# Two of a transformer block's branch projections as seven-product units, in place of plain products, in a one-core Trainium2 kernel

## The chip, the cores and the metric

The kernel runs on one core of a Trainium2 chip. The metric is the device time of one execution in microseconds (us), lower is better. The engines are called as the profile calls them: PE (TensorE, matrix products), PEld (its weight load), DVE (VectorE), ACT (ScalarE), POOL (GpSimd) and SP (SyncE, which here only issues transfers).

## The reference

One block of a streaming encoder on 256 positions of width 2048, in float32: a recurrence and a banded attention run side by side, their outputs are projected, gated and merged, and a squared-ReLU MLP follows. What matters here is the merge:

```python
z = u @ w_in                                   # u: rms_norm(x), 256 x 2048
...
gate_a, gate_b = jnp.split(jax.nn.sigmoid(gates), 2, axis=-1)
merged = gate_a * (y_a @ w_branch_a) + gate_b * (y_b @ w_branch_b)   # y: 256 x 1024, w_branch: 1024 x 2048
return merged @ w_out
...
h = h + jnp.square(jax.nn.relu(u @ w_up[l])) @ w_down[l]             # 2048 -> 8192 -> 2048
```

## The kernel before

Every matrix product is made from three fast ones. A weight tile `raw` of 128x1024 (two k tiles of 128 rows by 512 columns) comes from HBM, ACT casts its high part to `wh` (line 91), and DVE subtracts that to get the low part `wl` (line 92); the activations have been split in the same way. `mm3` (lines 140 to 142) then adds hi x wh, hi x wl and lo x wh into one PSUM bank. One such "split piece" therefore costs a load (issued by SP), a cast, a subtraction, and 12 matmuls of 128x512 (two k tiles, two halves m of the positions, three products each).

Large projections are made as a `Unit` of 1024 columns. In it 8 of the 16 k tiles are computed with seven block products in place of eight (a Strassen scheme): the weights' blocks A, B, C, D are combined on the way (`sums` on DVE: A+=B, later A+=C; `sent`: accumulating DMAs from POOL, B+=C and D+=A), and the activations' sums S2, S4, S5, S7 are made once by `combos`. Each of the seven products needs its own split piece, with only six matmuls per piece, since it serves one half m. The other k tiles are "plain" pieces with 12 matmuls, named `r<column half>_<k tile>`. A unit's four banks start from each other (`begun`: a copy on ACT), and two are corrected by `less` on DVE. `run` writes a unit's order; a unit's last plain pieces (`late`) run in the next unit, and the steps of other work (`steps`) are called at set places in it.

A piece is named after its unit, product and k tile: `gb0p11D0` is unit gb0, bank 11, block D, k tile 0; `gb0r1_8` is a plain piece. The order of the stages around the change is: gates `ga0`, `ga2` (with the attention's steps), gates `gb0`, `gb2`, the branches (`ba`, `bb`), the output projection `wo0`, `wo2`, the MLP's units `up00` to `up32` and `dn00` to `dn32`. The branches have 8 k tiles only. They are computed by `gemm2` in four rounds of 512 columns, for each round `ba` then `bb`, with four pieces of 12 matmuls each. DVE multiplies each result with its gate (line 1113), and adds the two (line 1124).

Program order is a proposal: a scheduler puts instructions of each engine into their final order by priorities (`tc.high_priority`), and each engine then runs its own list strictly in that order. So a waiting instruction holds everything behind it on that engine, and on SP or POOL every later transfer. Buffers: six `raw`, three `rawp`, two `rawd`, four each of `wh` and `wl`. From gb0 on there is a fifth `wh` and `wl` (`buf`, lines 204 to 207).

Of the kernel before, what the change touches and what calls it, by code (L numbers as in the profile page):

```python
# [50 lines left out]
def tile_hybrid_block(  # L51
# [5 lines left out]
    nc = tc.nc  # L57
# [86 lines left out]
    def lhs_of(lhs, kt, m):  # L144
        return [lhs[kt // 4][:, kt % 4, u, m * P:(m + 1) * P] for u in range(2)]
# [51 lines left out]


    homes = {}
    taken = {"wh": 0, "wl": 0}  # L200

    def buf(tag, what):

        if "fifth" in homes:
            taken[tag] += 1
        last = taken[tag] > 0 and taken[tag] % 5 == 0
        return (homes["fifth"] if last else wpool).tile([P, 2 * NC], F32R, name=f"{tag}_{what}", tag=tag, bufs=1 if last else 4)

    def piece(w, what, n0, k0, tag="raw"):

# [529 lines left out]
    def fours(t):  # L740
        return t.rearrange("p (k t) -> p k t", t=P)
# [35 lines left out]
            nc.vector.tensor_tensor(dst, acc, dst, op=ALU.add)  # L777

    LATE = [(12, 13), (14, 15)]
    ITEMS = [(1, (8, 9)), (1, (10, 11)), (0, (8, 9)), (0, (10, 11)), (0, (12, 13)), (0, (14, 15))] + [(1, ks) for ks in LATE]  # L780

    class Unit:


        def __init__(self, lhs, S, w, n0, what, done, kt0=0, apart=NC, steps=lambda: (), start=5, fresh=None, held=False, tail=False):
            self.lhs, self.S, self.w, self.n0, self.what, self.done = lhs, S, w, n0, what, done
            self.apart = apart
            self.kt0, self.make_steps, self.start, self.held, self.tail = kt0, steps, start, held, tail
            self.spread, self.fresh = fresh is not None, fresh or ()
            self.raw, self.dma, self.c, self.items, self.steps = {}, {}, {}, list(ITEMS), []  # L790

        def load(self, name):

            jj, n, tag = {"A": (0, 0, "raw"), "B": (0, 1, "raw"), "C": (1, 1, "raw"), "D": (1, 0, "rawd")}[name]
            self.raw[name] = [piece(self.w, f"{self.what}{name}{g}", self.n0 + n * self.apart, self.kt0 + 4 * jj + g, tag)
                              for g in (0, 2)]

        def load_item(self):

# [23 lines left out]
                    mm3(self.c[i], *left(g + a), wh[:, a], wl[:, a], first and not g + a, False)  # L823

        def block(self, m, jj):
            return lambda k: lhs_of(self.lhs(), k + 4 * jj, m)

        def comb(self, i):
            return lambda k: self.S()[i][k]
# [31 lines left out]
        def plain(self, n, ks, which=range(NM)):  # L861

            while self.steps and self.steps[0][0] <= ks[-1] // 4:
                self.steps.pop(0)[1]()
            if (n, ks) not in self.raw:
                self.load_item()
            with ExitStack() as es:
                if marks and not n and ks in LATE:
                    es.enter_context(tc.issue_after(marks[0].ins))
                wh, wl = parts(self.raw[n, ks], f"{self.what}r{n}_{ks[0]}")  # L870

            def half(m, c=slice(0, NC)):
                for a, k in enumerate(ks):
                    mm3(self.c["12"[m] + "12"[n]][:, c], *lhs_of(self.lhs(), k, m), wh[:, a, c], wl[:, a, c], False, k == KD - 1)

            for m in which:
                half(m)
            return half
# [16 lines left out]
    def run(u, then=None):  # L895

        def q():
            if late:
                late.pop(0)()

        def item(x):
            if x and x.items:
                x.load_item()

        if not u.raw:
            u.load("A")
            u.load("B")
            u.load("C")
            u.load("D")
        for _ in range(3 - sum(type(k) is tuple for k in u.raw)):  # L910
            item(u)
        at = iter(range(99))
        seconds = [lambda: u.product("12", "C", u.comb(4)), lambda: u.product("11", "D", u.block(0, 1))]
        if not late and not u.spread:
            seconds.reverse()
        u.bank("11")
        u.product("11", "A", u.block(0, 0), True)
        u.begun("21", "11")
# [12 lines left out]
        u.step(next(at))  # L931
        seconds[1]()
        with ExitStack() as es:
            if u.spread:
                es.enter_context(tc.issue_after(lows[-1].ins))
            u.sums("A", "C")
        u.sent("D", "A")
        u.step(next(at))
        u.plain(1, (8, 9))
        item(u)  # L940
        u.step(next(at))
        u.product("21", "A", u.comb(2))
        u1 = u.copy(token(f"u1_{u.what}"), "21")
        if then:
            with ExitStack() as es:
                if u.held:
                    es.enter_context(tc.issue_after(u.dma[0, (10, 11)].ins))
                then.load("A")
        u.step(next(at))
        u.plain(1, (10, 11))  # L950
        u.less("12", u1)
        u.residual("12")
        item(u)
        u.step(next(at))
# [17 lines left out]
        if then:  # L972
# [10 lines left out]
        u.plain(0, (12, 13))  # L983
        item(u)
        u.step(next(at))
        u.plain(0, (14, 15))
# [12 lines left out]


# [66 lines left out]

    ga, gb = [], []
    units = []
    for gates, c, col, what, fresh in ((ga, 0, C_GA, "ga", None), (ga, 2, C_GA, "ga", None), (gb, 0, C_GB, "gb", ("21",)), (gb, 2, C_GB, "gb", ())):  # L1070
# [254 lines left out]
```

## Time and profile before

| | us |
|---|---|
| median of three runs (lowest, highest) | 1368.17 (1367.55, 1371.06) |
| the profiled execution | 1367.7 |
| its span, first to last instruction | 1366.0 |
| PE busy | 1356.6 (99 %) |
| DVE, ACT, POOL busy | 1122.2, 948.5, 150.1 |
| mean granted TensorE clock | 0.998 |

A row of the busy-time part names an engine, its busy time, its share of the span and its number of instructions. A row of the windows view gives one stretch: its length, then for each engine busy time and number of instructions, the granted clock, the share of the DMA engines' time and the bytes per second. A row of the timeline gives start, duration, engine, line, operation, output and inputs, and in brackets how long the engine sat idle before it and what ended that. A matmul's shown duration (about 390 ns) overlaps the next one, so the distance of two starts is what a matmul costs; the same holds, by less, for DVE and ACT.

### The profile page before, as it was taken

The page shows a single profiled execution, that of the slowest core. Times are in us where ns is not written, and L with a number is a line of the kernel's source. Part 1 is how long each engine was busy: PE and PEld are TensorE (multiplying, and loading weights), DVE is VectorE, ACT ScalarE, POOL GpSimd, SP SyncE. Part 2 cuts the span into 40 slices and gives each one's busy share as a digit, 9 for nine tenths or more (in the row PEclk, how much of TensorE's full clock was granted, in tenths as well). Part 3 has the DMA queues.
Part 4 walks back from the last instruction along what each step waited for, and adds up shares of the span by engine and source line. Part 5 has one row for each costly group of instructions (what it writes and reads, how often), then busy time and mean ns, then how long its engine had stood idle before and what let it go on. Part 6 is the DMA issues. An engine that isn't in the chain of part 4 may idle for free.

```text
span 1366.0 us, 19039 instructions
## 1 busy us (share of the span) xinstructions
PE 1356.6 (99%) x6787; PEld 1123.0 (82%) x6787; DVE 1122.2 (82%) x1302; ACT 948.5 (69%) x1247; POOL 150.1 (11%) x231
## 2 busy tenths in 40 slices
PE   9999999999999999999999999999999999999997
PEld 8888888878778888888888888888888888888886
DVE  7888977887788775798998987789787888878885
ACT  6877765776777664456678766687666876668864
POOL 4000000111111000010121111100111002110210
PEclk9999999999999999999999999999999999999999
DMA  9655557788886996569899889998899888998892
GB/s 333 240 186 156 181 177 264 216 221 244 260 225 169 293 296 210 182 154 324 284 265 269 235 260 295 283 256 244 250 278 298 250 253 237 286 296 258 269 281 98
DMA packets 128895, 333.75 MB, mean 244 GB/s; under 512 B 11152, under 2 KB 12176, under 8 KB 128416
## 3 DMA queue, kind: packets, MB, share of 16 engines
q1 hardware_dynamic: 108080, 265.85, 56.2%
q0 software_dynamic: 20144, 66.14, 24.7%
q8 instruction: 53, 0.87, 0.2%
q10 hardware_dynamic: 576, 0.55, 0.1%
q14 instruction: 42, 0.34, 0.1%
HBM read 271.67 MB, written 10.49 MB: 207 GB/s over the span
## 4 chain that ended last, share of the span: by engine, by line
PE 99%; DMA 1%; ACT 0%; POOLq 0%; issue 0%; POOL 0%
PE acc_hq L182 2%; PE acc_hf L182 2%; PE tp_u L110 1%; PE acc_hg L142 1%; PE acc_hi L142 1%; PE acc_hg L140 1%; PE acc_bb L140 1%; PE acc_hi L141 1%; PE acc_hf L187 1%; PE acc_ba L142 1%; PE acc_hg L141 1%; PE acc_bb L142 1%; PE acc_ba L140 1%; PE acc_ba L141 1%; PE acc_hi L140 1%; PE acc_bb L141 1%
## 5 line engine op out<-in xcount | busy, mean ns | idle before, releaser
L182 PE MATMUL acc_hf<-act_x,wh_hf 128*128 128x512 f32 x128 | 40.9, 401 | 0.6 <-ACT wh_hf L91 0.6
L182 PE MATMUL acc_hq<-act_x,wh_hq 128*128 128x512 f32 x128 | 40.8, 399 | 0.2 <-ACT wh_hq L91 0.2
L91 ACT CAST wh_bb<-raw_bb 128x1024 fp32r<-128x1024 f32 x16 | 16.9, 1054 | 23.3 <-PE acc_ba L142 17.7
L92 DVE TENSOR_TENSOR wl_bb<-raw_bb,wh_bb 128x1024 fp32r<-128x1024 f32 x16 | 19.6, 1223 | 14.8 <-ACT wh_bb L91 14.8
L91 ACT CAST wh_ba<-raw_ba 128x1024 fp32r<-128x1024 f32 x16 | 16.9, 1053 | 19.9 <-PE acc_bb L142 13.8
L92 DVE TENSOR_TENSOR wl_ba<-raw_ba,wh_ba 128x1024 fp32r<-128x1024 f32 x16 | 19.6, 1223 | 10.8 <-ACT wh_ba L91 10.8
L187 PEld LDWEIGHTS acc_hf<-act_x,wl_hf 128*128 128x128 f32 x128 | 23.4, 189 | 5.7 <-DVE wl_hf L92 0.5
L187 PEld LDWEIGHTS acc_hq<-act_x,wl_hq 128*128 128x128 f32 x128 | 23.4, 188 | 5.2
L1220 POOL DMA_DIRECT2D hd<-y x24 | 26.2, 1171 | 1.8 <-ACT y L1219 1.3
L92 DVE TENSOR_TENSOR act_u<-tp_u,act_u 128x512 fp32r<-128x512 f32 x32 | 21.9, 684 | 4.7 <-ACT act_u L91 4.2
L140 PE MATMUL acc_bb<-wh_bb,act_yb 128*128 128x512 f32 x64 | 25.2, 393 | 0.0
L140 PE MATMUL acc_hg<-wh_hg,act_x 128*128 128x512 f32 x64 | 25.1, 392 | 0.0
L140 PE MATMUL acc_hi<-wh_hi,act_x 128*128 128x512 f32 x64 | 25.0, 391 | 0.0
L142 PE MATMUL acc_hg<-wh_hg,act_x 128*128 128x512 f32 x64 | 24.9, 390 | 0.0
L142 PE MATMUL acc_ba<-wh_ba,act_ya 128*128 128x512 f32 x64 | 24.9, 389 | 0.0
L142 PE MATMUL acc_hi<-wh_hi,act_x 128*128 128x512 f32 x64 | 24.9, 389 | 0.0
L141 PE MATMUL acc_hi<-wl_hi,act_x 128*128 128x512 f32 x64 | 24.9, 389 | 0.0
L141 PE MATMUL acc_hg<-wl_hg,act_x 128*128 128x512 f32 x64 | 24.9, 389 | 0.0
L140 PE MATMUL acc_ba<-wh_ba,act_ya 128*128 128x512 f32 x64 | 24.9, 389 | 0.0
L141 PE MATMUL acc_ba<-wl_ba,act_ya 128*128 128x512 f32 x64 | 24.9, 389 | 0.0
L141 PE MATMUL acc_bb<-wl_bb,act_yb 128*128 128x512 f32 x64 | 24.9, 389 | 0.0
L142 PE MATMUL acc_bb<-wh_bb,act_yb 128*128 128x512 f32 x64 | 24.9, 389 | 0.0
(1996 smaller groups left out, 5220.2 us busy)
## 6 DMA issues: line engine op xcount, KB each, us to landing
raw_hi<-in_w_in_n_dram SPq DMA_DIRECT2D x16, 512.0 KB, 4.2
raw_hg<-in_w_in_n_dram SPq DMA_DIRECT2D x16, 512.0 KB, 3.6
raw_ba<-in_w_branch_a_dram SPq DMA_DIRECT2D x16, 512.0 KB, 4.5
raw_bb<-in_w_branch_b_dram SPq DMA_DIRECT2D x16, 512.0 KB, 4.5
raw_hf<-in_w_in_t_dram SPq DMA_DIRECT2D x12, 512.0 KB, 4.1
raw_hq<-in_w_in_t_dram SPq DMA_DIRECT2D x12, 512.0 KB, 5.3
hd<-y POOLq DMA_DIRECT2D x24, 256.0 KB, 7.5
raw_aq<-in_w_in_t_dram SPq DMA_DIRECT2D x8, 512.0 KB, 4.5
```

What stands on the lines that cost most here:

```text
L91: casts[:] = [(copy or nc.scalar.copy)(hi, src)]
L92: low[:] = [nc.vector.tensor_tensor(lo, src, hi.bitcast(F32), op=ALU.subtract)]
L110: nc.tensor.transpose(tp[:, j, :], src[:, j * P:(j + 1) * P], ident)
L140: nc.tensor.matmul(acc, hi, wh, start=first, stop=False, skip_group_check=True)
L141: nc.tensor.matmul(acc, hi, wl, start=False, stop=False, skip_group_check=True)
L142: newest[:] = [nc.tensor.matmul(acc, lo, wh, start=False, stop=last, skip_group_check=True)]
L182: newest[:] = [nc.tensor.matmul(acc[cb], wh[:, cb * P:(cb + 1) * P], r.rearrange("p u t -> p (u t)"), start=kt == 0, stop=last)]
L187: newest[:] = [nc.tensor.matmul(acc[cb][:, 0:T], wl[:, cb * P:(cb + 1) * P], r[:, 0, :], start=False, stop=False)]
L1220: nc.gpsimd.dma_start(hd[n][m], t, accum_op=ALU.add)
```

## The change

The first 1024 columns of both branches become two units, `ba0` and `bb0`, of a new small size (`nkt=8`): four k tiles by seven products, in two pairs, and four by plain pieces. Per unit that is 7 product pieces of 6 matmuls and 4 plain pieces of 12, so 90 matmuls where there were 96, and 11 split pieces where there were 8. `ba0` and `bb0` are chained behind `gb2` by `run`. The last 1024 columns stay with `gemm2`.

- The activations' sums for both branches are made ahead: eight additions of 128x256 on DVE (line 1077, a step of gb0) and four of 128x512; in gb2 four splits into S5, S4, S2 and S7 follow. They need a home for four tiles, `ysum`.
- That home is the place of the fifth `wh` and `wl`, which are gone. All units from gb0 to the end have four.
- The gated results of the first 1024 columns are summed by four accumulating DMAs from POOL (line 1116, 256 KB each) in place of four additions on DVE.
- The transposes of the first two merged blocks (`turned`) both come behind the third round's `ba`.

```diff
-        if "fifth" in homes:
-            taken[tag] += 1
-        last = taken[tag] > 0 and taken[tag] % 5 == 0
-        return (homes["fifth"] if last else wpool).tile([P, 2 * NC], F32R, name=f"{tag}_{what}", tag=tag, bufs=1 if last else 4)
+        return wpool.tile([P, 2 * NC], F32R, name=f"{tag}_{what}", tag=tag, bufs=4)
...
+    ITEMS8 = [(1, (4, 5)), (0, (4, 5)), (0, (6, 7)), (1, (6, 7))]
...
             self.raw[name] = [piece(self.w, f"{self.what}{name}{g}", self.n0 + n * self.apart, self.kt0 + self.nkt // 4 * jj + g, tag)
                               for g in range(0, self.nkt // 4, 2)]
...
-        if not late and not u.spread:
+        if len(late) < 2 and not u.spread:
             seconds.reverse()
...
-        u.plain(1, (8, 9))
+        if not u.small:
+            u.plain(1, (8, 9))
...
-        u.plain(1, (10, 11))
+        u.plain(1, (4, 5) if u.small else (10, 11))
...
         if then:
             then.load("B")
             then.load("C")
+            if then.small:
+                then.load("D")
...
-        u.plain(0, (8, 9))
+        u.plain(0, (4, 5) if u.small else (8, 9))
...
-        u.plain(0, (10, 11))
+        u.plain(0, (6, 7) if u.small else (10, 11))
...
-            u.plain(1, LATE[1])
+            u.plain(1, (6, 7) if u.small else LATE[1])
...
+    def y_block(m, j):
+        a = ysums[m, j] = fours(homes["fifth"].tile([P, NC], F32, name=f"ysum{m}{j}", tag=f"raw5{'ABCD'[2 * m + j]}", bufs=1))
+        for i, y in enumerate((ya, yb)):
+            x = y[0][:, 2 * j:2 * j + 2, :, m * P:(m + 1) * P].bitcast(F32)
+            nc.vector.tensor_tensor(a[:, 2 * i:2 * i + 2], x[:, :, 0, :], x[:, :, 1, :], op=ALU.add)
+
+    def y_final(i):
+        if not y_steps:
+            y_steps.extend(combos(None, "y", tk, Sy, ysums))
+        y_steps[i]()
...
+                              lambda: [(KD, lambda i=i: y_final(i), at) for i, at in enumerate((3, 5, 7, 9))]) if c else (
+                              lambda: [(KD, lambda m=m, j=j: y_block(m, j), 5 + 2 * m + j) for m in range(NM) for j in range(2)]),
...
+    def gated(what):
+
+        def done(m, n, acc):
+            gate = (ga if what == "ba" else gb)[n][m]
+            nc.vector.tensor_tensor(gate, acc, gate, op=ALU.mult)
+            if what == "bb":
+                nc.gpsimd.dma_start(ga[n][m], gate, accum_op=ALU.add)
+
+        return done
+
+    for i, (y, w, what) in enumerate(((ya, w_branch_a, "ba"), (yb, w_branch_b, "bb"))):
+        units.append(Unit(lambda y=y: y, lambda i=i: {k: v[2 * i:2 * i + 2] for k, v in Sy.items()}, w, 0, f"{what}0", gated(what), nkt=8))
     for u, then in zip(units, units[1:] + [None]):
         run(u, then)
...
-    for n in range(4):
+    for n in range(2, 4):
...
-            if what == "ba" and n:
-                for _, f in turned(mT, n - 1, f"m{n - 1}", ga):
-                    f()
+            if what == "ba":
+                for i in range(2 if n == 3 else 0, n):
+                    for _, f in turned(mT, i, f"m{i}", ga):
+                        f()
```

The order that results differs at three places that matter below. The first is DVE at the start of unit gb0, from the second half of product 22A to the first plain piece r1_8. `raw_gb0A0<-raw_gb0A0,raw_gb0C0` is the sum A+=C. Before:

```order
L92 TENSOR_TENSOR wl_gb0p22A0_4490<-raw_gb0A0_4217,wh_gb0p22A0_4489 128x1024
L92 TENSOR_TENSOR wl_gb0p22A2_4500<-raw_gb0A2_4219,wh_gb0p22A2_4499 128x1024
L92 TENSOR_TENSOR wl_gb0p12C2_4524<-raw_gb0C2_4268,wh_gb0p12C2_4523 128x1024
L92 TENSOR_TENSOR wl_gb0p11D0_4534<-rawd_gb0D0_4349,wh_gb0p11D0_4533 128x1024
L92 TENSOR_TENSOR wl_gb0p11D2_4544<-rawd_gb0D2_4351,wh_gb0p11D2_4543 128x1024
L854 TENSOR_TENSOR raw_gb0A0_4217<-raw_gb0A0_4217,raw_gb0C0_4266 128x1024
L854 TENSOR_TENSOR raw_gb0A2_4219<-raw_gb0A2_4219,raw_gb0C2_4268 128x1024
L92 TENSOR_TENSOR wl_gb0r1_8_4558<-rawp_gb0r1_8_4396,wh_gb0r1_8_4557 128x1024
```

After (the eight additions of line 1077 stand further ahead, between the pieces 11A0 and 11A2, and the sum of line 759 behind them):

```order
L92 TENSOR_TENSOR wl_gb0p22A0_4490<-raw_gb0A0_4217,wh_gb0p22A0_4489 128x1024
L763 TENSOR_TENSOR ysum10_4675<-ysum00_4620,ysum10_4675 128x512
L92 TENSOR_TENSOR wl_gb0p22A2_4500<-raw_gb0A2_4219,wh_gb0p22A2_4499 128x1024
L764 TENSOR_TENSOR ysum00_4620<-ysum11_4694,ysum00_4620 128x512
L92 TENSOR_TENSOR wl_gb0p12C0_4514<-raw_gb0C0_4266,wh_gb0p12C0_4513 128x1024
L765 TENSOR_TENSOR ysum01_4653<-ysum01_4653,ysum00_4620 128x512
L92 TENSOR_TENSOR wl_gb0p12C2_4524<-raw_gb0C2_4268,wh_gb0p12C2_4523 128x1024
L92 TENSOR_TENSOR wl_gb0p11D0_4534<-rawd_gb0D0_4349,wh_gb0p11D0_4533 128x1024
L92 TENSOR_TENSOR wl_gb0p11D2_4544<-rawd_gb0D2_4351,wh_gb0p11D2_4543 128x1024
L850 TENSOR_TENSOR raw_gb0A0_4217<-raw_gb0A0_4217,raw_gb0C0_4266 128x1024
L850 TENSOR_TENSOR raw_gb0A2_4219<-raw_gb0A2_4219,raw_gb0C2_4268 128x1024
L92 TENSOR_TENSOR wl_gb0r1_8_4558<-rawp_gb0r1_8_4396,wh_gb0r1_8_4557 128x1024
```

Three of the four combining additions (`ysum`) stand between the subtractions, and 12C0, which before came ahead of 22A0, stands behind 22A2.

The second place is DVE in unit up00, from the subtraction of piece 11D2 to that of the first plain piece r1_8. `hw` and `act_h` are the normed MLP input of the blocks 2 and 3, scaled out of a transpose (`tp`) and then split. Before:

```order
L92 TENSOR_TENSOR wl_up00p11D2_6670<-rawd_up00D2_6473,wh_up00p11D2_6669 128x1024
L854 TENSOR_TENSOR raw_up00A2_6331<-raw_up00A2_6331,raw_up00C2_6401 128x1024
L92 TENSOR_TENSOR act_h2_6618<-hw_2_0_6624,act_h2_6618 128x4x128
L1150 TENSOR_TENSOR hw_2_1_6654<-tp_h21_6649,vt_76 128x512
L92 TENSOR_TENSOR wl_up00r1_8_6695<-rawp_up00r1_8_6510,wh_up00r1_8_6694 128x1024
L92 TENSOR_TENSOR wl_up00p21A0_6723<-raw_up00A0_6329,wh_up00p21A0_6722 128x1024
```

After:

```order
L92 TENSOR_TENSOR wl_up00p11D2_6734<-rawd_up00D2_6537,wh_up00p11D2_6733 128x1024
L850 TENSOR_TENSOR raw_up00A0_6393<-raw_up00A0_6393,raw_up00C0_6463 128x1024
L92 TENSOR_TENSOR act_h2_6682<-hw_2_0_6688,act_h2_6682 128x4x128
L1181 TENSOR_TENSOR hw_2_1_6718<-tp_h21_6713,vt_76 128x512
L850 TENSOR_TENSOR raw_up00A2_6395<-raw_up00A2_6395,raw_up00C2_6465 128x1024
L92 TENSOR_TENSOR act_h2_6682<-hw_2_1_6718,act_h2_6682 128x4x128
L1181 TENSOR_TENSOR hw_3_0_6753<-tp_h30_6748,vt_76 128x512
L92 TENSOR_TENSOR wl_up00r1_8_6759<-rawp_up00r1_8_6574,wh_up00r1_8_6758 128x1024
```

The first sum A+=C has moved behind 11D2 (before, it stood right behind 22A0), and the second half of `act_h2` and the first of block 3 now stand ahead of r1_8. On PE the transposes of block 3 (`tp_h30`) stand ahead of r1_8 in both; after one matmul for each of r1_8's two banks, `tp_h31` comes, which before had come behind all twelve.

The third place is SP, the queue of loads, in the branches. Before, where the branches' rounds had only plain loads:

```order
L216 DMA raw_ba10_5249<-in_w_branch_a_dram 128x2x512
L216 DMA raw_ba12_5267<-in_w_branch_a_dram 128x2x512
L216 DMA raw_ba14_5285<-in_w_branch_a_dram 128x2x512
L216 DMA raw_ba16_5303<-in_w_branch_a_dram 128x2x512
L216 DMA raw_bb10_5340<-in_w_branch_b_dram 128x2x512
L216 DMA raw_bb12_5358<-in_w_branch_b_dram 128x2x512
L216 DMA raw_bb14_5376<-in_w_branch_b_dram 128x2x512
```

After, in unit bb0 (`ba2`, `bb2` are the third round):

```order
L211 DMA rawp_bb0r1_4_5279<-in_w_branch_b_dram 128x2x512
L211 DMA rawp_bb0r0_4_5283<-in_w_branch_b_dram 128x2x512
L211 DMA rawd_wo0D0_5873<-in_w_out_dram 128x1024
L211 DMA rawp_bb0r0_6_5285<-in_w_branch_b_dram 128x2x512
L211 DMA raw_ba26_5521<-in_w_branch_a_dram 128x2x512
L211 DMA raw_bb20_5573<-in_w_branch_b_dram 128x2x512
L211 DMA rawp_bb0r1_6_5320<-in_w_branch_b_dram 128x2x512
L211 DMA raw_bb22_5591<-in_w_branch_b_dram 128x2x512
```

The last plain piece of bb0, `rawp_bb0r1_6`, stands behind `raw_ba26` and `raw_bb20`, whose buffers are those that bb0's blocks A and B leave: the first is free when the accumulating DMA D+=A has read it, and the second when product 21B has been split.

More of the change, by code (lines that the diff above doesn't have):

```diff
@@ L199, in tile_hybrid_block @@
     homes = {}
-    taken = {"wh": 0, "wl": 0}
     def buf(tag, what):
-        if "fifth" in homes:
-            taken[tag] += 1
-        last = taken[tag] > 0 and taken[tag] % 5 == 0
-        return (homes["fifth"] if last else wpool).tile([P, 2 * NC], F32R, name=f"{tag}_{what}", tag=tag, bufs=1 if last else 4)
+        return wpool.tile([P, 2 * NC], F32R, name=f"{tag}_{what}", tag=tag, bufs=4)
     def piece(w, what, n0, k0, tag="raw"):
@@ L779, in tile_hybrid_block, with __init__ @@
     LATE = [(12, 13), (14, 15)]
+    ITEMS8 = [(1, (4, 5)), (0, (4, 5)), (0, (6, 7)), (1, (6, 7))]
     ITEMS = [(1, (8, 9)), (1, (10, 11)), (0, (8, 9)), (0, (10, 11)), (0, (12, 13)), (0, (14, 15))] + [(1, ks) for ks in LATE]
     class Unit:
-        def __init__(self, lhs, S, w, n0, what, done, kt0=0, apart=NC, steps=lambda: (), start=5, fresh=None, held=False, tail=False):
+        def __init__(self, lhs, S, w, n0, what, done, kt0=0, apart=NC, steps=lambda: (), start=5, fresh=None, held=False, tail=False, nkt=KD):
             self.lhs, self.S, self.w, self.n0, self.what, self.done = lhs, S, w, n0, what, done
-            self.apart = apart
+            self.apart, self.nkt, self.small = apart, nkt, nkt < KD
             self.kt0, self.make_steps, self.start, self.held, self.tail = kt0, steps, start, held, tail
             self.spread, self.fresh = fresh is not None, fresh or ()
-            self.raw, self.dma, self.c, self.items, self.steps = {}, {}, {}, list(ITEMS), []
+            self.raw, self.dma, self.c, self.items, self.steps = {}, {}, {}, list(ITEMS if nkt == KD else ITEMS8), []
         def load(self, name):
             jj, n, tag = {"A": (0, 0, "raw"), "B": (0, 1, "raw"), "C": (1, 1, "raw"), "D": (1, 0, "rawd")}[name]
-            self.raw[name] = [piece(self.w, f"{self.what}{name}{g}", self.n0 + n * self.apart, self.kt0 + 4 * jj + g, tag)
-                              for g in (0, 2)]
+            self.raw[name] = [piece(self.w, f"{self.what}{name}{g}", self.n0 + n * self.apart, self.kt0 + self.nkt // 4 * jj + g, tag)
+                              for g in range(0, self.nkt // 4, 2)]
         def load_item(self):
@@ L825, in block @@
         def block(self, m, jj):
-            return lambda k: lhs_of(self.lhs(), k + 4 * jj, m)
+            return lambda k: lhs_of(self.lhs(), k + self.nkt // 4 * jj, m)
         def comb(self, i):
@@ L873, in half @@
                 for a, k in enumerate(ks):
-                    mm3(self.c["12"[m] + "12"[n]][:, c], *lhs_of(self.lhs(), k, m), wh[:, a, c], wl[:, a, c], False, k == KD - 1)
+                    mm3(self.c["12"[m] + "12"[n]][:, c], *lhs_of(self.lhs(), k, m), wh[:, a, c], wl[:, a, c], False, k == self.nkt - 1)
             for m in which:
@@ L971, in run @@
         u.residual("21")
-        if then:
+        if then and not then.small:
             then.load("D")
@@ L982, in run @@
         u.step(next(at))
[L983 to L986, printed above, removed]
+        if not u.small:
+            u.plain(0, (12, 13))
+            item(u)
+            u.step(next(at))
+            u.plain(0, (14, 15))
         marks.clear()
@@ L993, in rest @@
         def rest():
-            u.plain(1, LATE[1])
+            u.plain(1, (6, 7) if u.small else LATE[1])
             u.end(1)
-        late.append(lambda: u.plain(1, LATE[0]))
+        if not u.small:
+            late.append(lambda: u.plain(1, LATE[0]))
         late.append(rest)
@@ L1069, in tile_hybrid_block @@
     units = []
+    ysums, Sy, y_steps = {}, {}, []
+    def y_block(m, j):
[7 more added lines that the diff above has]
+        y_steps[i]()
     for gates, c, col, what, fresh in ((ga, 0, C_GA, "ga", None), (ga, 2, C_GA, "ga", None), (gb, 0, C_GB, "gb", ("21",)), (gb, 2, C_GB, "gb", ())):
@@ L1075, in done @@
             gates[c + n][m] = sigmoid(token(f"gate_{what}{c + n}{m}", tkb if what == "gb" else None), acc, m)
-        units.append(Unit(lambda: xT, lambda: Sx, w_in_t, col + c * NC, f"{what}{c}", done, steps=gate_steps.pop(0) if gate_steps else lambda: (), fresh=fresh, held=what == "gb" and not c))
+        units.append(Unit(lambda: xT, lambda: Sx, w_in_t, col + c * NC, f"{what}{c}", done,
+                          steps=gate_steps.pop(0) if gate_steps else (
+                              lambda: [(KD, lambda i=i: y_final(i), at) for i, at in enumerate((3, 5, 7, 9))]) if c else (
+                              lambda: [(KD, lambda m=m, j=j: y_block(m, j), 5 + 2 * m + j) for m in range(NM) for j in range(2)]),
+                          fresh=fresh, held=what == "gb" and not c))
     for i in range(2):
```

## Prediction

> **What bounds the kernel now.** I read the busy shares first, then the chain that ended last, then what PE waited for.
>
> ```profile
> PE 1356.6 (99%) x6787; PEld 1123.0 (82%) x6787; DVE 1122.2 (82%) x1302; ACT 948.5 (69%) x1247; POOL 150.1 (11%) x231
> PE 99%; DMA 1%; ACT 0%; POOLq 0%; issue 0%; POOL 0%
> PE ps_warm L81 <- DVE warm L79: 1.1, 1, 1.1
> PE acc_hf L182 <- ACT wh_hf L91: 0.6, 1, 0.6
> PE acc_hq L182 <- ACT wh_hq L91: 0.2, 1, 0.2
> ```
>
> PE is busy 99 % of the span, carries 99 % of the chain, and waited 1.9 us in all, at the very start. A matmul less is therefore time gained, if nothing new makes PE wait. Whether PE waits depends on how far DVE and ACT are ahead of it in making `wh` and `wl`. The windows show how full they are, from the gates' first units with the attention (250:420) to the MLP:
>
> ```profile
> 250.00:420.00 170.00, 169.99 (x838) 135.91 (x836) 141.13 (x161) 125.19 (x199) 20.26 (x34) 1.00 0.84 244
> 420.00:436.00 16.00, 16.00 (x81) 12.78 (x80) 11.73 (x12) 12.76 (x15) 1.75 (x2) 1.00 0.58 155
> 436.00:450.00 14.00, 14.00 (x63) 11.45 (x62) 12.71 (x12) 9.72 (x12) 1.69 (x2) 1.00 0.64 134
> 450.00:513.00 63.00, 63.00 (x280) 52.16 (x279) 46.16 (x41) 40.59 (x45) 3.38 (x4) 1.00 0.90 301
> 513.00:600.00 87.00, 87.00 (x398) 72.32 (x397) 62.55 (x72) 38.46 (x43) 1.38 (x2) 1.00 0.61 190
> 640.00:680.00 40.00, 40.00 (x185) 33.08 (x185) 38.35 (x44) 30.14 (x41) 6.21 (x11) 1.00 0.94 297
> 680.00:712.00 32.00, 32.00 (x151) 26.47 (x150) 31.55 (x37) 23.74 (x33) 6.83 (x9) 1.00 0.85 242
> 712.00:1366.00 654.00, 646.55 (x2923) 535.03 (x2921) 536.36 (x513) 464.66 (x570) 79.92 (x101) 1.00 0.89 258
> ```
>
> DVE (the third busy time) has 24 us free in the branches (513:600), 1.3 of 14 at the start of gb0, and 2.1 of 72 from 640 to 712. The last two are the tight places.
>
> **What it removes.** Two units lose 6 matmuls each. What one costs is read where ACT's casts follow the release of buffers, one plain piece of 12 matmuls apart:
>
> ```profile
> 516.48 1.05 ACT L91 CAST wh_bb<-raw_bb 128x1024 fp32r<-128x1024 f32 x1 [1.09 <-PE acc_ba L142]
> ...
> 530.08 1.05 ACT L91 CAST wh_ba<-raw_ba 128x1024 fp32r<-128x1024 f32 x1 [1.67 <-PE acc_bb L142]
> ```
>
> These are the first and last of six in a row: 13.60 us for 5 x 12 matmuls, 0.2267 us each. So 12 fewer are worth -2.72 us; that is the most that can be gained. (The Trainium skill, page "TensorE: Matmul & The Clock Gate", section "Back-to-back issue gap", gives columns / 2.4 GHz + 2.5 ns, 0.216 us for 512 columns; by that it would be -2.59 us. The row here is 5 % above it, and the sum goes by the row.)
>
> **What it adds in the branches.** The durations:
>
> ```profile
> L91 ACT CAST wh_ba<-raw_ba 128x1024 fp32r<-128x1024 f32 x16 | 16.9, 1053 | 19.9 <-PE acc_bb L142 13.8
> L92 DVE TENSOR_TENSOR wl_ba<-raw_ba,wh_ba 128x1024 fp32r<-128x1024 f32 x16 | 19.6, 1223 | 10.8 <-ACT wh_ba L91 10.8
> L842 DVE TENSOR_TENSOR acc_gb2c<-acc_gb2c,u_gb 128x512 f32<-128x512 f32 x2 | 1.4, 700 | 1.1 <-ACT u_gb L812 0.6 <-PE acc_gb2c L142 0.5
> L704 DVE TENSOR_TENSOR sb<-sb,rs 128x256 f32<-128x256 f32 x8 | 3.4, 422 | 0.2
> 437.56 0.57 ACT L812 COPY acc_gb0c<-acc_gb0c 128x512 f32<-128x512 f32 x1 [0.36 <-PE acc_gb0c L142]
> ```
>
> DVE gets 6 subtractions (7.3 us), 4 sums of the same size (4.9) and 4 corrections (2.8), and loses 4 additions of like size (2.7): +12.3, on 62.55 of 87 us. ACT gets 6 casts and 8 copies, 6 x 1.05 + 8 x 0.57 = +10.9, on 38.46. Both stay under 90 % of what is then 84 us, so PE covers them: 0. If a piece were late there, it would cost its own lateness once.
>
> The four gate sums by DMA are issued from bb0's end on, and their readers, the transposes, now stand behind the third round's `ba`, 48 matmuls or 10.9 us later. A like transfer is the 512 KB sum of 4.4 to 8.6 us, so it is covered; the transposes' buffers add perhaps 0.1.
>
> New is the queue on SP: bb0's last plain piece is loaded only behind `ba26`, which waits for the accumulating DMA D+=A.
>
> ```profile
> raw_bb<-in_w_branch_b_dram SPq DMA_DIRECT2D x16, 512.0 KB, 4.5
> L216 SPq DMA_DIRECT2D raw_ba<-in_w_branch_a_dram x16: 367/368/378, 479.7 to 563.2; - x16
> rawd_gb0D<-raw_gb0A POOLq DMA_DIRECT2D x2, 512.0 KB, 6.1
> rawd_gb2D<-raw_gb2A POOLq DMA_DIRECT2D x2, 512.0 KB, 8.6
> ```
>
> From bb0's product 11D, about when D+=A can go, to r1_6 PE has 66 matmuls, 15.0 us. Needed are 6.1 (gb0's, with DMA engines 0.6 busy as here) to 8.6 (gb2's, at 0.90), two issues of 0.37 on SP (the second row: shortest, median, longest, in ns), 4.5 for the load, and 1.05 + 1.22 for the split: 13.7 to 16.2. So between 1.3 of room and 1.2 late; I take 0.4.
>
> **What it adds in gb0.** Eight additions of 128x256 and four of 128x512 come onto DVE between 11A0 and r1_8. Back to back an operation costs less than its duration: one of 128x512 shows 0.68 and starts 0.60 ahead of the next (697.87 and 698.47, rows of up00 below), and so I estimate 0.42 - 0.08, say 0.33, for 128x256. 8 x 0.33 + 4 x 0.60 = 5.0 us.
>
> ```profile
> 423.09 1.22 DVE L92 TENSOR_TENSOR wl_gb0p11A<-raw_gb0A,wh_gb0p11A 128x1024 fp32r<-128x1024 f32 x1 [0.58 <-ACT wh_gb0p11A L91]
> 428.06 1.23 DVE L92 TENSOR_TENSOR wl_gb0p11A<-raw_gb0A,wh_gb0p11A 128x1024 fp32r<-128x1024 f32 x1 [0.76 <-ACT wh_gb0p11A L91]
> 433.50 1.23 DVE L92 TENSOR_TENSOR wl_gb0p22A<-raw_gb0A,wh_gb0p22A 128x1024 fp32r<-128x1024 f32 x1 [1.82 <-ACT wh_gb0p22A L91]
> 437.24 1.23 DVE L92 TENSOR_TENSOR wl_gb0p11D<-rawd_gb0D,wh_gb0p11D 128x1024 fp32r<-128x1024 f32 x1 [0.24 <-ACT wh_gb0p11D L91]
> 438.38 2.35 DVE L854 TENSOR_TENSOR raw_gb0A<-raw_gb0A,raw_gb0C 128x1024 f32<-128x1024 f32 x2
> 440.65 1.22 DVE L92 TENSOR_TENSOR wl_gb0r<-rawp_gb0r,wh_gb0r 128x1024 fp32r<-128x1024 f32 x1
> 442.84 0.39 PE L140 MATMUL acc_gb0c<-wh_gb0r,act_x 128*128 128x512 f32 x1
> ```
>
> Between the two pieces of 11A and 11D DVE idled 0.76 + 1.82 + 0.24 = 2.8 us, so r1_8's subtraction starts about 2.2 later, at 442.85, and is ready at 444.05. PE wants it at 442.84 + 0.23, and in the new order one hi x wh product of the other bank comes first, so at 443.3. That is 0.75 late; 0.8 with the hand-offs. Below: if the first idle stretch (0.58, ahead of 11A0) helps, 0.3. Above: if only the 1.82 is usable, 1.9. Behind r1_8 wait the subtractions of 21A on DVE, whose PE turn comes 12 matmuls on; they are not late for a second time. In gb2 four splits of 128x512 (0.68 us on DVE each) stand ahead of plain pieces where DVE has about 17 of 63 us free: 0.2, between 0 and 0.5.
>
> **What goes away: the fifth buffers.** From gb0 on a cast may start one piece later. A piece lasts 1.36 us (six matmuls) to 2.72 us, and its split takes 2.3 us, so a piece is late only where DVE has a queue. The window 250:420 is the same scheme with four buffers, with DVE at 83 % and ACT at 74 %, and PE idled 0.01 us in 170. The units behind 712 have DVE at 82 % and ACT at 71 %: 0 there. At the start of wo0, where the transposes' splits join in, 0.2 (0 to 0.5), and in the last unit 0.2 (0 to 0.5).
>
> **What is moved in up00.** DVE has no room here:
>
> ```profile
> 697.87 0.68 DVE L1150 TENSOR_TENSOR hw<-tp_h,vt 128x512 f32<-128x512 f32 x1
> 698.47 1.21 DVE L92 TENSOR_TENSOR wl_up00r<-rawp_up00r,wh_up00r 128x1024 fp32r<-128x1024 f32 x1
> 699.62 0.60 PE L110 MATMUL tp_h<-ident,h 128*128 128x128 f32 x4
> 699.97 0.48 PE L140 MATMUL acc_up00c<-wh_up00r,act_h 128*128 128x512 f32 x1
> 700.28 0.40 PE L141 MATMUL acc_up00c<-wl_up00r,act_h 128*128 128x512 f32 x1
> ```
>
> Before, r1_8's `wl` was ready at 699.68, 0.60 ahead of its use at 700.28. In the new order `hw` of block 3 stands ahead of it, and that reads the transposes `tp_h30`, whose matmuls begin at 699.62 and end at 700.22. Then 0.60 for `hw` and 1.22 for the subtraction: ready at 702.04. PE has two hi x wh products (0.45), the transposes `tp_h31` (0.35) and one product of 21A (0.23) to fill in, from 699.97 to 701.0. That is 1.0 late; I take 1.2, since `act_h` and a cast that ACT now makes later stand ahead as well. Below 0.5, if PE gets to the transposes earlier against DVE; above 2.2, if 21A's subtraction, behind two more operations of 0.60, is late too.
>
> **Sum.** -2.72 + 0.1 (transposes) + 0.4 (load of r1_6) + 0.8 (gb0) + 0.2 (gb2) + 0.4 (four buffers) + 1.2 (up00) = +0.4 us. The profiled execution took 1367.7 us (span 1366.0), so 1368.1; the median of the runs before, 1368.17, is 0.5 above the profiled one, and I keep 1368.1 as the time. What a measurement of this kernel can tell from no change is 0.3 %, 4.1 us; the whole gain lies within it.
>
> **Rivals.**
>
> *All is hidden.* The scheduler's order fits, and the small waits are not there: -2.7 to -2.0, so 1365.0 to 1365.7. For it speaks that PE idles nowhere in the trace, though DVE is at 99 % from 680 to 712; against it, that the lead at the two tight places is 1.2 and 0.60 us and the additions are larger. Chance 0.30.
>
> *Slower: the four buffers.* Behind the branches come 18 units (wo, up, dn). In each, eight product pieces stand in a row, 10.9 us of PE against 8 subtractions and 4 sums of 1.14 us from start to start (437.24 and 438.38), 13.7 of DVE. The lead from the plain pieces pays the 2.8 us, and with a buffer less the lead that can be held is smaller. If each unit then waits 0.4 us, that is 7.2, with the sum above 1375.3. It decides the sign from (4.1 - 0.4) / 18 = 0.2 us a unit. Against it: the window 250:420. For it: those units carry evictions that the earlier ones have not. Chance 0.11.
>
> *Slower: one transfer.* D+=A of bb0 takes 8.6 us and the load of r1_6 more than 4.5, as loads do in gb2, and PE stands for 3 us and more. The trace shows what the clock does when PE has little to do:
>
> ```profile
> 1355.00:1362.00 7.00, 3.55 (x22) 2.99 (x20) 3.07 (x7) 3.89 (x10) 1.13 (x4) 0.95 0.51 180
> 1362.00:1366.00 4.00, 0.00 (x0) 0.00 (x0) 0.00 (x0) 0.00 (x0) 0.00 (x0) 0.50 0.58 209
> ```
>
> Granted was 0.95, then 0.50, behind PE's last work. At half clock each 3 us of matmuls takes 3 more, so a wait of 3 to 3.5 us would cost some 6: 1373 to 1374. (The Trainium skill, the same page, section "What's actually happening", says that the clock halves after an idle window of about 3.4 us and returns after a busy one as long; no PE wait inside the kernel here is long enough to show it.) Chance 0.04.
>
> **How the numbers follow.** My forecast, small waits that give back about the gain, has 0.55, and its own range is 1365.8 to 1371.9 (each term at its lower, then at its upper end, the sum runs from -1.9 to +4.2). All hidden has 0.30, the two slower cases 0.15. The range that leaves out half of the slow cases and the lowest tail is 1365.0 to 1372.5. Faster by over 0.3 %, under 1364.1, is more than the 12 matmuls can give: 0.02. Slower by over 0.3 %, above 1372.3: 0.14. Within: 0.84.
>
> **What would show it.** PE's busy time and count fall by 12 matmuls between 503 and 600, with PE without idle there: the part is right. A PE wait for `wl_gb0r` of about 0.8 us near 443 and one for `wl_up00r` of about 1.2 near 698 show the two main terms; none there means that all is hidden. A wait for `wh_bb0r` shows the queue on SP; waits for `wl` of up and dn units, many and small, show the buffers. The forecast would be wrong above all if such waits recur in every unit.

## The result, and the profile after

The changed kernel takes 1380.68 us (median of five runs, 1378.05 to 1381.62) against 1368.43 before (1367.55 to 1371.06): the ratio is 1.0084, 95 % interval 1.0073 to 1.0095. It is 12.3 us slower, above the whole predicted range. The profiled execution has a span of 1379.9 us, 13.9 above that of before. The medians given below leave out two single executions: one of 3486.8 us of *plain loads ahead*, and one of 1507.83 us of the kernel before beside *sums later*.

The page's busy times and chain, and what PE waited for from ga2 on (waits of 0.4 us and more: total, times, longest):

```profile
PE 1360.5 (99%) x6775; PEld 1118.6 (81%) x6775; DVE 1138.0 (82%) x1328; ACT 959.6 (70%) x1265; POOL 155.5 (11%) x239
PE 50%; DMA 9%; DVE 4%; issue 4%; ACT 2%; POOL 1%; SPq 0%; POOLq 0%; ACTq 0%; DVEq 0%
DMA rawp_up10r<-in_w_up_dram 2%; DMA rawp_dn22r<-in_w_down_dram 1%; DMA rawp_dn12r<-in_w_down_dram 1%; DMA rawp_up30r<-in_w_up_dram 1%; PE acc_dn00c L142 1%; PE acc_dn00c L140 1%; PE acc_dn32c L141 1%; PE acc_dn32c L140 1%; PE acc_up02c L142 1%; PE acc_dn32c L142 1%; PE acc_wo0c L142 1%; PE acc_wo0c L141 1%; PE acc_up02c L140 1%; PE acc_wo0c L140 1%; PE acc_dn00c L141 1%
PE acc_dn30c L140 <- ACT u_dn L808: 1.4, 1, 1.4
PE acc_up10c L141 <- DVE wl_up10r L92: 1.2, 3, 0.8
PE acc_ga2c L140 <- ACT u_ga L808: 1.0, 1, 1.0
PE acc_up00c L141 <- DVE wl_up00r L92: 0.9, 1, 0.9
PE acc_dn02c L141 <- DVE wl_dn02r L92: 0.8, 2, 0.6
PE acc_up00c L141 <- DVE wl_up00p22A L92: 0.8, 1, 0.8
PE acc_up30c L141 <- DVE wl_up30r L92: 0.8, 1, 0.8
PE acc_up20c L141 <- DVE wl_up20r L92: 0.6, 1, 0.6
PE acc_gb0c L140 <- ACT acc_gb0c L808: 0.4, 1, 0.4
```

PE issued its 12 matmuls less, but its share of the chain fell from 99 % to 50 %: the chain now runs through loads of plain pieces (`rawp`) of up and dn units. Many of the waits are for a plain piece's `wl`, far behind the change. They are small, and a matmul's shown duration hides part of each, so PE's busy time rose by 3.9 us though it did less.

Where the time went is best read from each unit's length, the distance from its first matmul to the next unit's first matmul in the one profiled execution of each kernel (us; the branches, from gb2's first matmul to the end of `bb2`, are one row, because the units overlap there; the units from gb0 on that are not listed differ by less than 0.1, but for dn22, 0.35 longer after the change):

| | before | after | four buffers alone | plain loads ahead | fifth from wo2 | sums in gate slots | sums later |
|---|---|---|---|---|---|---|---|
| ga2 | 47.72 | 49.61 | 47.93 | 47.73 | 49.19 | 47.71 | 48.64 |
| gb0 | 35.68 | 36.45 | 36.41 | 36.88 | 36.59 | 37.03 | 35.68 |
| gb2 to bb2 | 113.30 | 111.60 | 114.34 | 111.83 | 111.62 | 110.69 | 110.67 |
| wo0 | 36.33 | 36.51 | 36.51 | 36.52 | 36.51 | 36.32 | 36.33 |
| up00 | 42.71 | 45.04 | 44.13 | 44.17 | 43.99 | 42.71 | 42.71 |
| dn02 | 40.80 | 41.69 | 41.61 | 40.80 | 40.80 | 40.80 | 40.80 |
| up10 | 40.80 | 43.05 | 42.11 | 40.80 | 40.80 | 40.80 | 40.80 |
| up12 | 42.83 | 43.29 | 43.33 | 42.81 | 42.83 | 42.81 | 42.83 |
| dn12 | 40.80 | 41.46 | 40.80 | 40.80 | 40.80 | 40.80 | 40.80 |
| up20 | 40.80 | 42.23 | 41.89 | 40.80 | 40.80 | 40.80 | 40.80 |
| up22 | 42.81 | 43.25 | 43.31 | 42.81 | 42.83 | 42.81 | 42.83 |
| up30 | 40.80 | 42.49 | 42.23 | 40.80 | 40.80 | 40.80 | 40.80 |
| up32 | 42.80 | 43.25 | 43.31 | 42.81 | 42.81 | 42.80 | 42.81 |
| dn30 | 42.71 | 44.40 | 44.39 | 44.23 | 42.73 | 42.71 | 42.73 |

The columns behind "after" are experiments told below. The branches are 1.7 us shorter after the change; from up00 to dn30 12.6 us are lost. ga2's 1.9 us are not the change's: PE's wait in ga2, between 410 and 420, comes ahead of the first instruction that stands otherwise (an ACT cast at 425.50), and *plain loads ahead*, which has the changed order there too, has 47.73.

One of the late plain pieces, in up10, by the timeline. First the kernel before: the first of D+=A's two transfers on POOL; SP's loads of the next unit's B, of r0_12, and of r0_14 with r1_12; ACT's casts of r0_12 and r0_14.

```profile
860.99 0.86 POOL L859 DMA_DIRECT2D rawd_up10D<-raw_up10A  x1 [7.12 <-DVE wl_up10p11D L92]
868.98 5.63 SPq L216 DMA_DIRECT2D raw_up12B<-in_w_up_dram  x2
874.71 0.42 SPq L216 DMA_DIRECT2D rawp_up10r<-in_w_up_dram  x1
876.33 1.55 SPq L216 DMA_DIRECT2D rawp_up10r<-in_w_up_dram  x2
880.44 1.05 ACT L91 CAST wh_up10r<-rawp_up10r 128x1024 fp32r<-128x1024 f32 x1 [1.07 <-DMA rawp_up10r<-in_w_up_dram]
884.33 1.05 ACT L91 CAST wh_up10r<-rawp_up10r 128x1024 fp32r<-128x1024 f32 x1 [2.83 <-DMA rawp_up10r<-in_w_up_dram]
```

The same after; the last two rows are what SP waited for (total, times, longest), before between 836 and 896, after between 840 and 900.

```profile
868.50 0.85 POOL L855 DMA_DIRECT2D rawd_up10D<-raw_up10A  x1 [0.61 <-DVE wl_up10p11D L92]
878.01 5.59 SPq L211 DMA_DIRECT2D raw_up12B<-in_w_up_dram  x2
883.69 0.42 SPq L211 DMA_DIRECT2D rawp_up10r<-in_w_up_dram  x1
885.35 1.94 SPq L211 DMA_DIRECT2D rawp_up10r<-in_w_up_dram  x2
890.01 1.05 ACT L91 CAST wh_up10r<-rawp_up10r 128x1024 fp32r<-128x1024 f32 x1 [4.71 <-DMA rawp_up10r<-in_w_up_dram]
893.91 1.05 ACT L91 CAST wh_up10r<-rawp_up10r 128x1024 fp32r<-128x1024 f32 x1 [2.85 <-DMA rawp_up10r<-in_w_up_dram]
SPq L216 <- DMA rawd_up10D<-raw_up10A: 8.1, 2, 4.8
SPq L211 <- DMA rawd_up10D<-raw_up10A: 11.0, 2, 6.2
```

up10's first matmul is at 851.38 before and at 855.87 after. Against it, D+=A goes 9.6 us in before and 12.6 after, since the pieces that it waits for are split later with four buffers; the next unit's B loads, whose buffers D+=A frees, hold SP until 23.2 and 27.7; and r0_12, behind them in SP's order, is loaded 23.3 and 27.8 us in. Its cast comes 29.1 and 34.1 us in. PE came to the piece 35.4 us in before (its first matmul at 886.74); a cast and a subtraction are 2.3. Before there were 4 us to spare, after PE waits. Already before, both casts waited for a load and not for a free `wh`, so any delay of the loads went straight into this lead.

### The profile page after: what moved, and what is told of

Same layout as the page of the kernel before. It is cut to its first block, busy times and chain, and to the rows that moved or that the text cites. A ratio compares the mean times of both kernels' runs of the same rounds, so it can differ in the third digit from the quotient of the medians.

```text
span 1379.9 us, 19077 instructions
## 1 busy us (share of the span) xinstructions
PE 1360.5 (99%) x6775; PEld 1118.6 (81%) x6775; DVE 1138.0 (82%) x1328; ACT 959.6 (70%) x1265; POOL 155.5 (11%) x239
## 4 chain that ended last, share of the span: by engine, by line
PE 50%; DMA 9%; DVE 4%; issue 4%; ACT 2%; POOL 1%; SPq 0%; POOLq 0%; ACTq 0%; DVEq 0%
DMA rawp_up10r<-in_w_up_dram 2%; DMA rawp_dn22r<-in_w_down_dram 1%; DMA rawp_dn12r<-in_w_down_dram 1%; DMA rawp_up30r<-in_w_up_dram 1%; PE acc_dn00c L142 1%; PE acc_dn00c L140 1%; PE acc_dn32c L141 1%; PE acc_dn32c L140 1%; PE acc_up02c L142 1%; PE acc_dn32c L142 1%; PE acc_wo0c L142 1%; PE acc_wo0c L141 1%; PE acc_up02c L140 1%; PE acc_wo0c L140 1%; PE acc_dn00c L141 1%
## 5 line engine op out<-in xcount | busy, mean ns | idle before, releaser
L187 PEld LDWEIGHTS acc_hf<-act_x,wl_hf 128*128 128x128 f32 x128 | 23.2, 188 | 5.8 <-DVE wl_hf L92 0.7
L92 DVE TENSOR_TENSOR wl_hf<-raw_hf,wh_hf 128x1024 fp32r<-128x1024 f32 (+2 forms) x21 | 20.4, 970 | 5.7 <-ACT wh_hf L91 5.6
L187 PE MATMUL acc_hf<-act_x,wl_hf 128*128 128x256 f32 x128 | 24.7, 280 | 0.0
L187 PE MATMUL acc_hq<-act_x,wl_hq 128*128 128x256 f32 x128 | 24.6, 279 | 0.0
L100 POOL TENSOR_TENSOR ro<-os,mhalf 128x4 f32<-128x4 f32 x4 | 4.4, 1098 | 166.5 <-DVE os L99 163.5
L92 DVE TENSOR_TENSOR wl_hg<-raw_hg,wh_hg 128x1024 fp32r<-128x1024 f32 x16 | 19.4, 1215 | 3.0 <-ACT wh_hg L91 3.0
L182 PEld LDWEIGHTS acc_hf<-act_x,wh_hf 128*128 128x128 f32 x128 | 19.8, 189 | 1.6 <-DVE wh_hf L91 1.1
L695 ACT ACTIVATE sb<-sb,mx 128x128 f32<-128x128 f32 (+1 forms) x32 | 14.3, 449 | 9.6 <-DVE mx L692 9.4
L182 PEld LDWEIGHTS acc_hq<-act_x,wh_hq 128*128 128x128 f32 x128 | 19.8, 189 | 0.9 <-ACT wh_hq L91 0.4
L1240 ACT ACTIVATE r<-r 128x512 f32<-128x512 f32 x32 | 20.2, 631 | 0.5
L92 DVE TENSOR_TENSOR wl_hq<-raw_hq,wh_hq 128x1024 fp32r<-128x1024 f32 (+2 forms) x21 | 20.2, 970 | 0.4 <-ACT wh_hq L91 0.2
```

The costliest lines, as they stand in the source:

```text
L92: low[:] = [nc.vector.tensor_tensor(lo, src, hi.bitcast(F32), op=ALU.subtract)]
L100: nc.gpsimd.tensor_tensor(dst, ms, mhalf[:, :width], op=ALU.pow)
L182: newest[:] = [nc.tensor.matmul(acc[cb], wh[:, cb * P:(cb + 1) * P], r.rearrange("p u t -> p (u t)"), start=kt == 0, stop=last)]
L187: newest[:] = [nc.tensor.matmul(acc[cb][:, 0:T], wl[:, cb * P:(cb + 1) * P], r[:, 0, :], start=False, stop=False)]
L695: nc.scalar.activation(s[:, j, d], s[:, j, d], AF.Exp, bias=mx[:, b, j:j + 1], accum_out=sums[:, b, j:j + 1])
L1240: nc.scalar.activation(t, t, AF.Square)
```

## The experiments

Theory 1 was that chain of transfers; theory 2 the mechanism of the prediction's slower rival, DVE's lead through eight product pieces; theory 3 that the new units upset what follows.

**Four buffers alone.** The kernel before, with this edit and nothing else:

```diff
-        if "fifth" in homes:
-            taken[tag] += 1
-        last = taken[tag] > 0 and taken[tag] % 5 == 0
-        return (homes["fifth"] if last else wpool).tile([P, 2 * NC], F32R, name=f"{tag}_{what}", tag=tag, bufs=1 if last else 4)
+        return wpool.tile([P, 2 * NC], F32R, name=f"{tag}_{what}", tag=tag, bufs=4)
```

> The kernel before with the fifth wh and wl taken away and nothing else changed. Theory 1 (loads): without the fifth buffers each product piece is split some 3 us later against PE, so the accumulating transfer D+=A goes later, SP stands on the next unit's B loads that wait for it, and the plain loads behind them come late; PE waits in the up and dn units. Theory 2 (DVE): with a buffer less DVE cannot hold its lead through eight product pieces. By both the time is 1368.4 + 12 to 15, so 1380 to 1383, with the losses in up00, up10, up20, up30 and the dn units. Theory 3 (the branches): the new units' transfers and additions upset what follows; by it this kernel takes 1368 to 1370.

1381.25 us, 1.0086 of before (1.0073 to 1.0099). The lost buffer alone costs as much as the whole change did; theory 3 falls as the cause of the loss. Its column also has +0.73 in gb0 and +1.04 in gb2 to bb2, where there are no branch sums at all. From wo2's first matmul on, the order of every engine and queue is the same here as after the change, up00's included, so what is lost there is lost by the four buffers and the order that the scheduler makes for them. Even so the two columns differ by up to 0.9 us in a unit (9.3 against 12.6 us from up00 to dn30): that is how far one profiled execution can be read.

**Plain loads ahead.** The changed kernel, where in the up and dn units the next unit's B loads are issued behind r0_12 and r0_14:

```diff
         if then:
-            then.load("B")
+            with ExitStack() as es:
+                if u.what[:2] in ("up", "dn"):
+                    es.enter_context(tc.issue_after(u.dma[0, (14, 15)].ins))
+                then.load("B")
             then.load("C")
```

> The changed kernel, four buffers, where in the up and dn units the next unit's B loads are issued behind the unit's own plain loads r0_12 and r0_14; the order of PE, DVE, ACT and POOL is the same row by row. Theory 1: the waits for r0_12 and r0_14 go, which are most of the 11 us lost from up00's end on: 1371 to 1375. Theory 2: SP's order does not matter, 1379.5 to 1382.

1372.25 us, 1.0024 (1.0014 to 1.0035): 8.4 us less than the changed kernel, with four buffers and with the order of PE, DVE, ACT and POOL unchanged. So most of the loss is SP's order behind a late transfer, theory 1, and theory 2 fails as the main cause. Here is up10 again, POOL, SP and ACT (its first matmul is at 852.88):

```profile
864.33 0.95 POOL L855 DMA_DIRECT2D rawd_up10D<-raw_up10A  x1
867.91 10.58 SPq L211 DMA_DIRECT2D rawp_up10r<-in_w_up_dram  x3
878.54 0.46 SPq L211 DMA_DIRECT2D raw_up12B<-in_w_up_dram  x1
883.00 1.05 ACT L91 CAST wh_up10r<-rawp_up10r 128x1024 fp32r<-128x1024 f32 x1 [1.18 <-PE acc_up10c L142]
885.72 1.05 ACT L91 CAST wh_up10r<-rawp_up10r 128x1024 fp32r<-128x1024 f32 x1 [1.67 <-PE acc_up10c L142]
```

Three plain loads, those of r0_12 and r0_14 among them, are ahead of `raw_up12B`, and the casts wait for PE to free a `wh`, no longer for a load. D+=A still goes late, 11.4 us in: 1.8 of the 3.0 us that it lost after the change come with the four buffers themselves, and the rest with the late pieces of the unit before. The column shows 40.80 for up10, up20, up30, dn02 and dn12. What is left is 1.2 in gb0, 1.2 in gb2 (against the last column), 1.5 in up00 and 1.5 in dn30; for the first three theory 2 is not excluded.

dn30 has, by the trace, the same cause on other queues (no run moves this load alone). There ACT must scale `wf`, the final norm's weights, ahead of a copy that PE waits for, and `wf`'s load stands on POOL behind D+=A. After:

```profile
1295.74 0.85 POOL L855 DMA_DIRECT2D rawd_dn30D<-raw_dn30A  x1 [1.96 <-DVE wl_dn30p11D L92]
1296.28 0.87 POOL L1297 DMA_DIRECT2D wf<-in_norm_final_w_dram  x1
1306.97 1.91 ACT L1298 ACTIVATE wf<-wf 128x2048 f32<-128x2048 f32 x1 [1.92 <-DMA wf<-in_norm_final_w_dram]
1308.79 0.56 ACT L808 COPY u_dn<-acc_dn30c 128x512 f32<-128x512 f32 x1
```

Before, ACT was not idle ahead of that scaling:

```profile
1280.72 0.85 POOL L859 DMA_DIRECT2D rawd_dn30D<-raw_dn30A  x1 [0.89 <-DMA raw_dn32A<-in_w_down_dram]
1281.25 0.88 POOL L1266 DMA_DIRECT2D wf<-in_norm_final_w_dram  x1
1292.74 1.91 ACT L1267 ACTIVATE wf<-wf 128x2048 f32<-128x2048 f32 x1
```

**Fifth back after the branches.** The place of the branch sums is handed back:

```diff
     tkb_cm.__exit__(None, None, None)
+    fifth_cm.__exit__(None, None, None)
+    homes["five"] = ctx.enter_context(tc.tile_pool(name="five", bufs=1, reuse_waits="tile"))
```

with `buf` as it was before, counting from there on.

> The changed kernel, with the fifth wh and wl given back from wo0 on, in the place that the branch sums leave. Theories 1 and 2: the losses behind the branches go, 1380.7 - 12 to 14, so 1366.5 to 1369. Theory 3: 1379 to 1381.

1371.97 us, 1.0020 (1.0012 to 1.0029). The up and dn units are all within 0.2 us of their old lengths, but the range was missed: gb2 to bb2 is 115.68 us, 4.1 more than after the change. ACT at bb0 shows why:

```profile
535.13 1.05 ACT L91 CAST wh_wo0p11D<-rawd_wo0D 128x1024 fp32r<-128x1024 f32 x1 [5.18 <-DMA rawd_wo0D<-in_w_out_dram]
536.09 1.04 ACT L91 CAST wh_bb0p22A<-raw_bb0A 128x1024 fp32r<-128x1024 f32 x1
```

The scheduler put wo0's split, two rounds early, ahead of bb0's, and its load held ACT and DVE. (That the free buffer made it do so is likely, but not shown.)

**Sums in gb2.** That kernel, with the eight additions of line 1077 held back into gb2 (steps of gb2, and `tc.issue_after(lows[-1].ins)` around each).

> The kernel with the fifth buffers back from wo0 on, and the eight additions of the branch sums held back from gb0's tight start into gb2. If they cost about 0.8 us in gb0, as the prediction had it, it is 0.3 to 1.0 us faster than the kernel with the fifth back alone, and gb0's length is back near 35.7 us from 36.5; if they were hidden, the two are the same within 0.3 us.

1376.62 us, 1.0059 (1.0045 to 1.0073), so slower, not faster. It carries the same early split of wo0, for which ACT stood idle 8.25 us here, so the total says nothing of the additions. gb0 says more: 36.37 us without them and 36.41 in the kernel with four buffers alone, against 36.45 after the change and 36.88 in *plain loads ahead*, which has the same order. With four buffers the additions cost gb0 between nothing and 0.5 us.

**Fifth from wo2.** The fifth pair is handed back at the same place, but `buf` counts from unit wo2 on.

> The changed kernel with the fifth wh and wl given back only from unit wo2 on. In the run before this one (fifth back from wo0 on) DVE's order had the subtraction of wo0p11D, which waits for its load, ahead of bb0's 22A; here it stands behind bb3. If that order was what cost bb0 its 4 us, the losses stay only in gb0 (0.7) and gb2 (1.0), where four buffers are left, against the 2.7 gained: 1367 to 1368.5, and bb0 is without a wait. If the handing back itself costs it, 1371 to 1373 again.

1369.51 us, 1.0003 (0.9993 to 1.0012). bb0's waits are gone, so the early split was the cause. The median is 1.0 us above the expected range: 1.3 us stay in up00, and ga2 had its 1.5 in this execution.

**Sums in the gate slots.** Five buffers throughout, as before the change. The four branch sums lie where gb2's gates are written later:

```diff
-        a = ysums[m, j] = fours(homes["fifth"].tile([P, NC], F32, name=f"ysum{m}{j}", tag=f"raw5{'ABCD'[2 * m + j]}", bufs=1))
+        a = ysums[m, j] = fours(token(f"ysum{m}{j}", tkb))
```

> The changed kernel with five wh and wl throughout as before; the branch sums lie in the slots of the gates of gb2, which are written only when the sums have been used. The branch units alone are left of the change. If the twelve matmuls are all that they bring and the additions in gb0 are hidden, before - 2.7 to - 2.2: 1365.8 to 1366.4, gb0 at 35.7 us. If the additions in gb0 cost 0.8, as the prediction had it, 1366.6 and gb0 at 36.4.

1366.71 us, 0.9988 (0.9979 to 0.9997), faster than before. Behind gb0 nothing is lost, and gb2 to bb2 is 2.6 us shorter: the twelve matmuls. But gb0 is at 37.03, 1.35 above before, with one wait:

```profile
PE acc_gb0c L141 <- DVE wl_gb0p11D L92: 1.1, 1, 1.1
```

So with five buffers the additions do cost something there, and it is more than the 0.8 predicted.

**Sums later in gb0.** The same, with the additions behind 21B:

```diff
-            nc.vector.tensor_tensor(a[:, 2 * i:2 * i + 2], x[:, :, 0, :], x[:, :, 1, :], op=ALU.add)
+            with tc.issue_after(lows[-1].ins):
+                nc.vector.tensor_tensor(a[:, 2 * i:2 * i + 2], x[:, :, 0, :], x[:, :, 1, :], op=ALU.add)
```

> Five buffers throughout and the branch sums in the gates' slots, as in the run before, and the additions held behind gb0's product 21B, where DVE has idle time. With five buffers gb0 took 37.03 us with the additions at its start, against 35.68 before, with a wait of 1.1 us for wl of 11D. If the additions made that wait, gb0 is 35.7 us again, and the time is 1.3 us lower: 1365.2 to 1365.7, 0.9977 of before. If the wait has another cause (the transfers of gb0), gb0 stays at 37 and the time at 1366.7.

1366.42 us, 0.9977 (0.9968 to 0.9986). gb0 is at 35.68, as before, so the additions made that wait. The ratio is the one expected; the median is 0.7 above the range, in rounds in which the kernel before had 1369.46. This version beats both kernels.

## Why the prediction was wrong

- *Twelve matmuls, -2.72 us*: right. The last two experiments show -2.6 from gb2 to bb2. The new units themselves make no PE wait, and what is left for the gate sums, the load of `bb0r1_6` (0.4 in the sum) and gb2's splits is about 0.1. D+=A of bb0 took 5.5 us where 6.1 to 8.6 had been taken (and the terms listed there add up to 13.6 to 16.1, not 13.7 to 16.2). The formula of the Trainium skill that the prediction sets beside its row (page "TensorE: Matmul & The Clock Gate", section "Back-to-back issue gap") is stated there for an isolated matmul and not for a stream like this one; the sum did not use it.
- *The fifth buffers, "0 there" for the units behind 712*: this step failed, and it alone put the time outside the range. Its comparison, the window 250:420 with four buffers and PE idle 0.01 us, showed that DVE and ACT keep up. It did not show how much earlier than needed a piece's last reader lets go of its `raw` buffer. The step priced the buffers by the engines that fill them; they also set when sums are made, so when D+=A goes, and what stands behind it on SP and POOL. Measured: 12.7 us for the buffers alone; in the changed kernel 8.4 come back by SP's order. The prediction had found that chain, at bb0, where it costs nothing, and did not follow it into the up and dn units, where the DMA engines are 0.89 busy against 0.61 (its own windows). Nor was the window alike in this: in ga2, which begins in it, D+=A goes 4.5 us after the first matmul (383.92), and the first plain load behind the next unit's B loads is issued 17.6 us after it; in up10 after the change these are 12.6 and 27.8. The two rows of ga2, before:

```profile
388.44 0.85 POOL L859 DMA_DIRECT2D rawd_ga2D<-raw_ga2A  x1 [3.96 <-DVE wl_ga2p11D L92]
401.49 0.37 SPq L216 DMA_DIRECT2D rawp_ga2r<-in_w_in_t_dram  x1
```

- *Slower rival, the four buffers*: right in place and sign, and the sign that the prediction named for it, small waits for `wl` of up and dn units, is what came. At 0.11 it was far too unlikely, and it was wrong in mechanism: DVE's lead is not what made most of the waits, since they go with DVE's order untouched. Nor do all 18 units lose; up00, up10, up20, up30 and dn30 carry 9.4 of the 12.6 us.
- *gb0, 0.8*: the length came out (0.77) by luck, the reason did not. Four buffers cost 0.73 without the additions, and PE's wait there, in both kernels, is 0.4 for ACT's copy of a bank, not for `wl_gb0r`. In the changed kernel most of the additions fell into time in which DVE would have waited for casts (1.81 us ahead of 22A's second half with four buffers alone, 0.16 after the change). With five buffers they cost 1.35.
- *gb2, 0.2*: 1.0 with four buffers alone, at least five times the term, and again not from the splits put there.
- *up00, 1.2*: the wait for `wl_up00r` came, 0.9 us, with four buffers alone as after the change, and with five throughout neither it nor any loss. But DVE did not stand for the transposes, as the prediction had it: it had no idle time ahead of `hw`, so its own list was late. After:

```profile
702.82 0.68 DVE L1181 TENSOR_TENSOR hw<-tp_h,vt 128x512 f32<-128x512 f32 x1
703.42 1.21 DVE L92 TENSOR_TENSOR wl_up00r<-rawp_up00r,wh_up00r 128x1024 fp32r<-128x1024 f32 x1
```

up00 is 2.3 longer after the change and 1.4 with four buffers alone; the additional 0.9 is the wait of 0.8 for `wl_up00p22A`. *Fifth from wo2* has one of 0.7 for it, and is 1.3 longer with five buffers in up00. What makes that wait stays open.

- *One transfer, then the clock*: not seen. PE's longest wait after is 1.4 us, and the granted clock is 1.00 in every window read from 423 to 1366, so these runs cannot test the rule on the clock.

## What to carry to other kernels

A buffer's worth is not the time of the engine that fills it: follow what its earlier release lets start, through sums and transfers, to the in-order queue on which that transfer stands ahead of other loads. When an edit takes buffers from all later stages, read the lead of each kind of piece there and the releaser of its cast (a load or PE), not the busy share of DVE alone. A place to borrow is one whose owner comes later, as the gates' slots here.

## What the runs showed of the hardware

An accumulating transfer of 512 KB between two tiles, D+=A, took from 5.5 to 11.0 us from issue to landing in the same two kernels. The rows are the view of transfers: bb0 after the change (513 to 560), and up10 before (836 to 896) and after (840 to 900), medians where there are two. The DMA engines' share was 0.80 from 513 to 600 after the change, and around up10 0.98 before (851 to 892) and 0.95 after (856 to 899). The prediction's upper end for one, 8.6, was gb2's; the trace before already had 9.6 in up10.

```profile
rawd_bb0D<-raw_bb0A POOLq DMA_DIRECT2D x1, 512.0 KB, 5.5
rawd_up10D<-raw_up10A POOLq DMA_DIRECT2D x2, 512.0 KB, 9.6
rawd_up10D<-raw_up10A POOLq DMA_DIRECT2D x2, 512.0 KB, 11.0
```
